# One more weight buffer, pooled group 3 in front, and the end of layer 1 in another order

## The chip, the core and the metric

The kernel runs on one core of one Trainium2 chip, alone. The metric is device time of one execution in microseconds. Three plain runs of the kernel before were timed, and one more execution was recorded by the hardware profiler. TensorE is called PE, VectorE DVE, ScalarE ACT, GpSimd POOL and SyncE SP.

## What is computed

Two layers of a diffusion backbone over 256 latent tokens and 256 context tokens of width 1024. Only the latent stream comes out, so layer 1 needs no branches or experts for the context tokens. Cut to what matters:

```python
def token_mixer(h, hc, ...):                    # four branches, each 512 wide
    out_a = fourier_mix(f_in)
    out_b = global_attention(q_b, k_b, v_b, ...)
    out_c = window_attention(q_c, k_c, v_c, ...)    # "attention c"
    out_d = pool_mix(p_in, pool_w, pool_scale)      # four groups, windows 2, 4, 8, 16
    return branch_merge(h, (out_a, out_b, out_c, out_d), ...)

def pool_mix(u, pool_w, pool_scale):
    # per group: mean over a window of tokens minus the token itself, then a 128x128 matrix
    mixed = einsum('btgc,gce->btge', pooled, pool_w)
    return mixed.reshape(b, t, POOL_W) * pool_scale

def branch_merge(h, branches, w_branch, w_gate, b_gate, w_out):
    for i, br in enumerate(branches):
        merged += sigmoid(h @ w_gate[i] + b_gate[i]) * (br @ w_branch[i])
    return merged @ w_out

def moe_ffn(h, ...):                            # 16 experts, two picked per token
    for e in range(16):
        hid = silu(tok @ w1[e]) * (tok @ w3[e])
        out += combine[:, e] * (hid @ w2[e])

def trunk_layer(...):
    x = x + g1 * token_mixer(...)
    x = x + g2 * moe_ffn(...)
# after two layers: rms_norm(x, norm_f)
```

All inputs are float32. A matmul is made of three float16 ones: the operand is split into a high and a low half, and high x high, low x high and high x low are added up.

## The kernel before

**Weights.** Every weight comes in chunks of 128 partitions by 2048 float32, 1 MB. `Stream.fill` issues their loads on SP's queue as far ahead as buffers allow. `split` makes the float16 halves: the high one (`whi`) on ACT, L319, then the low one (`wlo`) on DVE, L323; PE's three matmuls of `mm3` are L580, L581 and L582. Attention weights use the four `stage` buffers. Expert weights go round `stage`, `NEXT[l]` buffers named `ext` in the pool of the expert stage, and in layer 1 one more place (`X1`).

**The mixer.** A layer projects the inputs of attention b, runs it with the Fourier branch and `gated(0)` as filler, then does the same for attention c. Attention works through units: `S` on PE (L792, L796), the maximum on DVE (L797), the exponential `E` on ACT (L811), the row sum and `P` on ACT and DVE (L824, L825), a transpose of P by a DMA on SP's queue (L772; tiles `pair` in layer 0, `pt` in layer 1), and `po` on PE (L840). Between the steps of a unit `next(fill)` takes a step of the filler, so the order in which the filler's generators are chained sets what stands beside which unit on every engine. The filler of attention c is `spread(gated(1), pool_front(), SPREAD[l])`, then `pool_back()`, then `gated(3)`. `gated(i)` is the merge of branch i: gate matmuls (L1013 is their ACT step) and branch matmuls for two column blocks at a time. `spread` takes a step of the second generator after every step (layer 0) or every second step (layer 1) of the first.

**The pooled branch.** `pool_group(g)` computes 128 features (24 matmuls, from `h` and one half chunk of `w_in`), copies them on ACT (L941, L942), adds shifted copies on DVE (L944, L947 once for each doubling of the window, L951, L953, L955) and splits the result into `pmH` (ACT, L319) and `pmL` (DVE, L321). `mix(g)` is three matmuls with the group's matrix and the scaling into `brH`, `brL` (L975, L976). `pmH` and `pmL` have three buffers each.

**The experts.** Tokens are dealt to 16 experts in slots of 96. For each expert `up` computes w1 and w3 products (two chunks each), `hidden` their gated product `sa` (ACT L1388, DVE L1389), `down` the w2 product `py`. In layer 1 the outputs of the first fourteen experts go to DRAM (`ydram`), and when expert 14 has begun to be worked off, `fetch` gathers the rows of each token back: four indirect DMAs issued by POOL (L1405), two for each of two token tiles. `combine(t)` weighs and adds the two rows: L1412 on ACT, L1413 on DVE, and with `gated` L1415 and L1416 on DVE, which add the result to the stream X. The last two experts are added from PSUM (`acc`, L1339; their inputs `yHL`). Expert 15 keeps `sa` and its w2 chunks in float32, so its `py` matmuls (L1318) start from `sa`. In layer 0 the gathers are eight. The descriptors of POOL's indirect DMAs are built in a scratch in SBUF, whose size is an argument of the program, 16 KB a partition if none is given.

Of the kernel before, what the change touches and what calls it, by code (L numbers as in the profile page):

```python
# [23 lines left out]
NE = 16  # L24
# [13 lines left out]
BIG = 4096.0  # L38
CH = 2048
NSTG = 4  # L40
NEXT = (7, 7)
WHOLE = ((15,), (15,))
RAW = ("ada", "raw")
NWSP = 3
# [243 lines left out]
def run_all(g):  # L288
    for _ in g:
        pass  # L290
# [17 lines left out]
class Kernel:  # L308
# [305 lines left out]
    def mixer(self, l, nq, side):  # L614
        nc, tc, A, W, wk, sm = self.nc, self.tc, self.A, self.W, self.wk, self.sm
        pe, act, dve = nc.tensor, nc.scalar, nc.vector
        C, LC, split, mm3 = self.C, self.LC, self.split, self.mm3
        full = nq == NTOK
# [1 line left out]
        hH, hL = self.h if full else self.norm_mod(l, 1, NTOK, 0, 2)  # L620
        scope = ExitStack()
        at = Pool(scope.enter_context(tc.tile_pool(name=f"att{l}", bufs=1)),
                  {"pmH": 3, "pmL": 3, "a2": 3, "P": 3, "pt": 2 - full, "E": 3, "G": 2})

        def feat_part(ps, w, sl, n, k0, k1):
            mm3(ps[:, 0:n], lambda k: w[0][:, k, sl], lambda k: w[1][:, k, sl],
# [301 lines left out]
        def pool_group(g):  # L928
            w = W.get("half", "w_in", (l,), 512 + g * 128)
            ps = self.mm()  # L930
            yield from feat(ps, w, slice(0, 128), nq, True)
            pH = at.tile([128, 512], F16, "pmH")
            pL = at.tile([128, 512], F16, "pmL")
            win = POOL_WINDOWS[g]
            e = win // 2
            for st in range(nst):
                buf = [at.tile([128, T + 16], F32, f"pool{i}") for i in range(2)]
                p0 = at.tile([128, T], F32, "poolp", tag="a2")
                dve.memset(buf[0][:, 0:8], 0.0)
                dve.memset(buf[0][:, T + 8:T + 16], 0.0)  # L940
                act.activation(buf[0][:, 8:T + 8], ps[:, st * T:st * T + T], AF.Copy, scale=AS * DS)  # L941
                act.activation(p0, ps[:, st * T:st * T + T], AF.Copy, scale=AS * DS)  # L942
                cur, hi, lo, d = 1, T + 16, 1, 1
                dve.tensor_tensor(buf[1][:, 1:hi], buf[0][:, 0:hi - 1], buf[0][:, 1:hi], op=ALU.add)  # L944
                for _ in range(g):
                    nlo, nhi = lo + d, hi - d
                    dve.tensor_tensor(buf[1 - cur][:, nlo:nhi], buf[cur][:, nlo - d:nhi - d],  # L947
                                      buf[cur][:, nlo + d:nhi + d], op=ALU.add)
                    cur, lo, hi, d = 1 - cur, nlo, nhi, d * 2
                sv = buf[cur][:, 8:T + 8]  # L950
                dve.tensor_tensor(sv[:, 0:e], sv[:, 0:e], C("invc", 16 * g, 16 * g + e), op=ALU.mult)  # L951
                if e > 1:
                    dve.tensor_tensor(sv[:, T - e + 1:T], sv[:, T - e + 1:T],  # L953
                                      C("invc", 16 * g + 8, 16 * g + 7 + e), op=ALU.mult)
                dve.scalar_tensor_tensor(p0, sv, 1.0 / win, p0, op0=ALU.mult, op1=ALU.subtract)  # L955
                split(pH[:, st * T:st * T + T], pL[:, st * T:st * T + T], p0, 1.0)
                yield
            pooled[g] = pH, pL

        def pool_front():  # L960
            pool_weights()
            for g in range(3):
                yield from pool_group(g)

        def pool_back():
            bH, bL = new_br(3)
            pwH, pwL = pooled["w"]
            psl = pooled["s"]

            def mix(g):  # L970
                pH, pL = pooled.pop(g)
                po = self.mm()
                mm3(po[:, 0:nq], lambda k: pwH[:, g, :], lambda k: pwL[:, g, :],
                    lambda k: pH[:, 0:nq], lambda k: pL[:, 0:nq], 1)
                act.activation(bH[:, g, 0:nq], po[:, 0:nq], AF.Copy, scale=psl[:, g:g + 1])  # L975
                dve.scalar_tensor_tensor(bL[:, g, 0:nq], po[:, 0:nq], psl[:, g:g + 1], bH[:, g, 0:nq],  # L976
                                         op0=ALU.mult, op1=ALU.subtract)

            mix(0)
            yield  # L980
            last = pool_group(3)
            for g in range(1, 3):
                next(last, None)
                mix(g)
                yield
            yield from last
            mix(3)
            pooled["done"] = True

        mg = self.lay.tile([128, KD, nq], F32, "merged")  # L990
# [43 lines left out]
        P = project("b", 1024)  # L1034
# [3 lines left out]
        P = project("c", 1792)  # L1038
# [7 lines left out]
        self.moe_scope = ExitStack()  # L1046
        self.mp = Pool(self.moe_scope.enter_context(tc.tile_pool(name=f"moe{l}", bufs=1)), {"Dg": 1 if full else 2, "ext": NEXT[l], "yHL": 2, "whi": MORE[l], "wlo": MORE[l]})
        self.next, self.spare, self.more = NEXT[l], int(not full), MORE[l]
        self.ext = self.mp
# [30 lines left out]
    def moe(self, l, nt, side):  # L1080
        nc, tc, A, wk, sm, mp = self.nc, self.tc, self.A, self.wk, self.sm, self.mp
# [165 lines left out]
        pe_all = ntt == 2  # L1247
# [4 lines left out]
        def experts(W, hot0, h2):  # L1252
# [133 lines left out]
            def hidden(e, pa, pb):  # L1386
                sa = wk.tile([128, 4, CAP], F32, "sa", tag="t2")
                act.activation(sa, pa, AF.Silu, scale=DS)  # L1388
                dve.scalar_tensor_tensor(sa, pb, AS * DS, sa, op0=ALU.mult, op1=ALU.mult)  # L1389
                if e in whole:  # L1390
                    return sa
                hd = [wk.tile([128, 4, CAP], F16, f"hd{i}", tag="t2") for i in range(2)]
                split(hd[0], hd[1], sa, 1.0)
                return hd
# [15 lines left out]
            def combine(t, gated=False):  # L1410
                y0, y1 = mid["yg", t]
                tc.keep_in_program_order(act.activation(y0, y0, AF.Copy, scale=wr[:, 0, t:t + 1]))  # L1412
                dve.scalar_tensor_tensor(y0, y1, wr[:, 1, t:t + 1], y0, op0=ALU.mult, op1=ALU.add)  # L1413
                if gated:
                    TT(y0, y0, mid["g2"][t // 2], op=ALU.mult)  # L1415
                    TT(xt(t), xt(t), y0, op=ALU.add)  # L1416
# [33 lines left out]
            prev = more = None  # L1450
            for e in range(NE):
                pa = up(e, "w1")
                if e == NE - 1 and pe_all:
                    combine(0, True)
                if more:
                    next(more, None)
                    next(more, None)
                if prev is not None:
                    down(e - 1, prev)
                if e == NE - 1 and pe_all:  # L1460
                    combine(1, True)
                if e == NE - 1 and not pe_all:
                    fetch()
                    dw = mid["dw"] = wk.tile([128, 4, 128], F32, "dw", tag="t2")
                    for t in range(2, 4):
                        for r in range(2):
                            dve.tensor_scalar(dw[:, 2 * t - 4 + r, :], C("ident"), wr[:, r, t:t + 1], AS,
                                              op0=ALU.mult, op1=ALU.mult)
                pb = up(e, "w3")
                if e == NE - 1 and pe_all:  # L1470
                    nf = self.ext.tile([128, CH], F32, "nf", tag="ext")[:, 0:D]
                    self.row_load(nf, A["norm_f"], D)
                if more:
                    run_all(more)
                    more = None
                if pe_all and e > early:
                    for t in range(ntt):
                        for half in range(2):
                            acc[t, half] = self.ps.tile([128, 512], F32, f"acc{t}{half}", tag=("mm", "pst")[half])
                    accumulate(e - 1)  # L1480
                prev = hidden(e, pa, pb)
                if e == 1:
                    index()
                if e % EPG == 1 and e // EPG < 3:
                    more = dispatch(e // EPG + 1)
                if e == 10:
                    side_rows()
                if e == early and pe_all:
                    fetch()
# [73 lines left out]
def build(inputs):  # L1563
    import concourse.bacc as _bacc

    nc = _bacc.Bacc("TRN2", target_bir_lowering=False, num_devices=1)
    orders = {}
    Kernel(Dry(), Dry(), Dry(), orders, dry=True).body()
    arrays, A = {}, {}
    arr, places = host_arrays(inputs, orders)  # L1570
    for name, a in arr.items():
        arrays[f"in_{name}_dram"] = a
        A[name] = nc.dram_tensor(f"in_{name}_dram", a.shape, mybir.dt.from_np(a.dtype), kind="ExternalInput").ap()
    out = nc.dram_tensor("out_0_dram", (1, T, D), F32, kind="ExternalOutput").ap()
    with tile.TileContext(nc) as tc:
        Kernel(tc, A, out, orders, places).body()
    return nc, arrays
# [8 lines left out]
```

## Time and profile before

| | us |
|---|---|
| plain runs, median (lowest to highest of 3) | 1464.87 (1464.43 to 1466.42) |
| the profiled execution | 1468.68 |
| its span, from first to last instruction | 1466.9 |
| PE busy | 1352.5 (92%) |
| DVE busy | 1119.0 (76%) |
| ACT busy | 953.2 (65%) |

Layer 0 ends at about 865 us of the span. Attention c ends at about 375 in layer 0 and at about 1085 in layer 1. The rows below give all times from the start of the span. A timeline row is: start, duration, engine, line, operation, tiles, shapes, number of instructions merged, and in brackets how long the engine was idle before and what ended that. The granted clock is a share of full speed: 1.00 is 2.4 GHz and 0.50 is 1.2 GHz.

### The profile page before, as it was taken

The numbers are of one execution on the slowest core, as the hardware profiler recorded it, in microseconds if no ns is written. First come the engines' busy times: TensorE is split into PE (matmuls) and PEld (weight loads), VectorE is DVE, ScalarE is ACT, GpSimd is POOL, SyncE is SP. The second block draws the span as 40 slices with busy tenths as digits, with TensorE's granted clock in tenths as the row PEclk, the third lists the DMA queues.
The fourth block names the chain that finished last, engine by engine and source line by source line (L and its number), as shares of the span: only waits on it lengthen the run. The fifth ranks groups of instructions, "written<-read, shape, count | busy, mean of one in ns | idle before, by whom it ended". The sixth has DMA issues, their size and how long they took to land. (4 is left out here: it accounts for less than half of the span.)

```text
span 1466.9 us, 33640 instructions
## 1 busy us (share of the span) xinstructions
PE 1352.5 (92%) x14151; PEld 927.0 (63%) x14151; DVE 1119.0 (76%) x2003; ACT 953.2 (65%) x1431; POOL 14.0 (1%) x16
## 2 busy tenths in 40 slices
PE   5999999998999998999999978899989989999984
PEld 3545454444444585777777747587768767777762
DVE  3887647877354557888988888868957888989986
ACT  3777535655233337889898655856845579899971
POOL 0000000000000000000000110000000000000010
PEclk9999999999899999999999999999999999999997
DMA  9559762797685337799999564774979779999981
GB/s 365 207 131 226 228 207 87 198 232 202 187 340 191 120 111 259 270 337 419 397 420 380 222 248 177 188 234 116 232 240 361 263 280 341 418 419 419 399 327 52
DMA packets 146416, 383.31 MB, mean 261 GB/s; under 512 B 91856, under 2 KB 93904, under 8 KB 108112
## 3 DMA queue, kind: packets, MB, share of 16 engines
q1 hardware_dynamic: 133136, 355.24, 68.8%
q10 hardware_dynamic: 11392, 19.56, 3.6%
q0 software_dynamic: 1728, 6.29, 1.2%
q8 instruction: 112, 1.84, 0.5%
q14 instruction: 48, 0.39, 0.1%
HBM read 344.88 MB, written 15.20 MB: 245 GB/s over the span
## 5 line engine op out<-in xcount | busy, mean ns | idle before, releaser
L580 PE MATMUL mm<-hH,whi 128*128 128x96 f16 (+2 forms) x1824 | 398.5, 261 | 3.3 <-ACT whi L319 2.6
L582 PE MATMUL mm<-hH,wlo 128*128 128x96 f16 (+2 forms) x1824 | 398.1, 261 | 1.0 <-DVE wlo L323 0.9
L323 DVE SCALAR_TENSOR_TENSOR wlo<-stage,whi 128x1024 f16<-128x1024 f32 (+1 forms) x212 | 318.9, 1522 | 105.0 <-ACT whi L319 104.3
L581 PE MATMUL mm<-hL,whi 128*128 128x96 f16 (+2 forms) x1824 | 398.2, 261 | 0.0
L580 PEld LDWEIGHTS <-whi 128*128 128x128 f16 x3104 | 304.9, 98 | 75.2 <-issue 4.4
L319 ACT ACTIVATE whi<-stage 128x1024 f16<-128x1024 f32 (+1 forms) x212 | 269.8, 1294 | 126.2 <-PE mm L581 87.1
L582 PEld LDWEIGHTS <-wlo 128*128 128x128 f16 x3104 | 305.0, 98 | 73.7 <-DVE wlo L323 2.7
L581 PEld LDWEIGHTS <-whi 128*128 128x128 f16 x3104 | 305.0, 98 | 72.2 <-issue 2.1
L323 DVE SCALAR_TENSOR_TENSOR wlo<-ext,whi 128x2048 f16<-128x2048 f32 x116 | 262.1, 2287 | 43.2 <-ACT whi L319 43.2
L319 ACT ACTIVATE whi<-ext 128x2048 f16<-128x2048 f32 x116 | 217.8, 1904 | 9.9 <-PE mm L582 7.4
L582 PE MATMUL mm<-xg,wlo 128*128 128x96 f16 x1024 | 132.3, 206 | 0.0
L580 PE MATMUL mm<-xg,whi 128*128 128x96 f16 x1024 | 132.3, 206 | 0.0
L581 PE MATMUL mm<-xg,whi 128*128 128x96 f16 x1024 | 132.3, 206 | 0.0
L581 PE MATMUL py<-wlo,hd 128*96 128x512 f16 x240 | 90.9, 379 | 8.9 <-DVE wlo L323 8.7
L582 PE MATMUL py<-whi,hd 128*96 128x512 f16 x240 | 90.2, 381 | 6.8 <-DVE hd L321 6.0
L580 PE MATMUL py<-whi,hd 128*96 128x512 f16 x240 | 91.0, 379 | 0.0
L580 PE MATMUL mm<-brH,whi 128*128 128x512 f16 (+1 forms) x256 | 83.5, 326 | 0.0
L582 PE MATMUL mm<-brH,wlo 128*128 128x512 f16 (+1 forms) x256 | 83.4, 326 | 0.0
L581 PE MATMUL mm<-brL,whi 128*128 128x512 f16 (+1 forms) x256 | 83.4, 326 | 0.0
L1270 PE MATMUL mm<-Dg,merged 128*128 128x384 f16 x384 | 70.3, 336 | 3.8 <-DVE Dg L1203 1.8
L500 PE MATMUL mm<-stage,cpad 128*32 128x256 f32 x768 | 58.5, 408 | 13.7 <-DMA stage<-in_w_ada_dram 13.6
L825 DVE SCALAR_TENSOR_TENSOR P<-E,rl,P 128x512 f16<-128x512 f32 (+1 forms) x96 | 59.2, 659 | 8.4 <-ACT P L824 8.2
(313 smaller groups left out, 2054.2 us busy)
## 6 DMA issues: line engine op xcount, KB each, us to landing
ext<-in_w_dram SPq DMA_DIRECT2D x118, 1024.0 KB, 9.3
stage<-in_w_dram SPq DMA_DIRECT2D x62, 1024.0 KB, 9.1
stage<-in_w_ada_dram SPq DMA_DIRECT2D x48, 1024.0 KB, 6.0
stage<-in_w_gate_dram SPq DMA_DIRECT2D x32, 1024.0 KB, 5.8
stage<-in_w_in_dram SPq DMA_DIRECT2D x16, 1024.0 KB, 6.7
stage<-in_w_branch_dram SPq DMA_DIRECT2D x32, 512.0 KB, 4.1
ydram<-ys ACTq DMA_DIRECT2D x56, 192.0 KB, 6.9
stage<-in_w_out_dram SPq DMA_DIRECT2D x8, 1024.0 KB, 6.1
```

What stands on the lines that cost most here:

```text
L319: a = nc.scalar.activation(hi, src, AF.Copy, scale=scale)
L323: b = nc.vector.scalar_tensor_tensor(lo, src, scale, hi, op0=ALU.mult, op1=ALU.subtract)
L500: pe.matmul(ps[32 * j:32 * j + 32, :], self.cpad[:, 2 * k:2 * k + 32], st[:, k, :], start=k < 4, stop=k >= 4, tile_position=(0, 32 * j))
L580: pe.matmul(ps, wH(k), xH(k), start=first and k == 0, stop=False)
L581: pe.matmul(ps, wH(k), xL(k), start=False, stop=False)
L582: pe.matmul(ps, wL(k), xH(k), start=False, stop=last and k == nk - 1)
L825: dve.scalar_tensor_tensor(pv[:, 1, qt, :], E[qt][:, 0:nk], r[:, qt:qt + 1], pv[:, 0, qt, :], op0=ALU.mult, op1=ALU.subtract)
L1270: pe.matmul(ps[:, 0:SLOTS], h2[n][t][:, cs(k)], Dg[:, t].rearrange("p e c -> p (e c)"), start=t == 0, stop=t == ntt - 1)
```

## The change

Three things are changed.

1. `NEXT` goes from 7 to 8 in both layers: one more `ext` buffer, 8 KB a partition. The scratch for the descriptors of indirect DMAs goes from 16 KB to 4 KB a partition. `pmH` and `pmL` get a fourth buffer each.
2. `pool_group(3)` moves from `pool_back` to `pool_front`. Its matmuls, copies and shifts now stand among the steps of `gated(1)`, and `pool_back` is four `mix` steps and nothing else.
3. In the last expert of layer 1 `combine(0)` stands behind `down(14)` instead of ahead of it, and `combine(1)` behind `hidden(15)` instead of ahead of the w3 product.

```diff
-NEXT = (7, 7)
+NEXT = (8, 8)
...
-                  {"pmH": 3, "pmL": 3, "a2": 3, "P": 3, "pt": 2 - full, "E": 3, "G": 2})
+                  {"pmH": 4, "pmL": 4, "a2": 3, "P": 3, "pt": 2 - full, "E": 3, "G": 2})
...
         def pool_front():
             pool_weights()
-            for g in range(3):
+            for g in range(4):
                 yield from pool_group(g)
...
-            mix(0)
-            yield
-            last = pool_group(3)
-            for g in range(1, 3):
-                next(last, None)
+            for g in range(4):
                 mix(g)
                 yield
-            yield from last
-            mix(3)
             pooled["done"] = True
...
                 pa = up(e, "w1")
-                if e == NE - 1 and pe_all:
-                    combine(0, True)
...
                     down(e - 1, prev)
                 if e == NE - 1 and pe_all:
-                    combine(1, True)
+                    combine(0, True)
...
                 prev = hidden(e, pa, pb)
+                if e == NE - 1 and pe_all:
+                    combine(1, True)
...
-    nc = _bacc.Bacc("TRN2", target_bir_lowering=False, num_devices=1)
+    nc = _bacc.Bacc("TRN2", target_bir_lowering=False, num_devices=1, dynamic_dma_scratch_size=4096)
```

PE, layer 0, the last score units of attention c. `S` is a score unit, `po` the product with v, `mm<-hH,whi` a gate matmul of branch 3. Before:

```order
L796 LDWEIGHTS qs
L796 MATMUL S<-kL_2761,qs 128x256
L792 LDWEIGHTS qs
L792 MATMUL S<-kH_2760,qs 128x256
L796 LDWEIGHTS qs
L796 MATMUL S<-kL_2761,qs 128x256
L840 LDWEIGHTS vH
L840 MATMUL po<-pair,vH 64x256
L840 LDWEIGHTS vH
L840 MATMUL po<-pair,vH 64x256
```

After:

```order
L792 LDWEIGHTS qs
L792 MATMUL S<-kH_2760,qs 128x256
L796 LDWEIGHTS qs
L796 MATMUL S<-kL_2761,qs 128x256
L580 LDWEIGHTS whi
L580 MATMUL mm<-hH,whi 128x512
L792 LDWEIGHTS qs
L792 MATMUL S<-kH_2760,qs 128x256
L796 LDWEIGHTS qs
L796 MATMUL S<-kL_2761,qs 128x256
L581 LDWEIGHTS whi
L581 MATMUL mm<-hL,whi 128x512
```

The unit on kH was followed by twelve po matmuls; it now has gate matmuls inside and behind it, and its po stand some hundred rows further down. The unit on kH_2762 that follows is interleaved in the same way.

DVE, layer 1, around the last P of attention c (`pool`, `poolp` and `pmL` are those of pooled group 3). Before:

```order
L1002 SCALAR_TENSOR_TENSOR merged<-gate,merged 128x256
L323 SCALAR_TENSOR_TENSOR wlo<-stage,whi 128x1024
L825 SCALAR_TENSOR_TENSOR P<-E,rl,P 128x512 x2
L944 TENSOR_TENSOR pool_19155<-pool_19154 128x271
L976 SCALAR_TENSOR_TENSOR brL_19114<-mm,psl,brH_19113 128x256
L947 TENSOR_TENSOR pool_19154<-pool_19155 128x269
L976 SCALAR_TENSOR_TENSOR brL_19114<-mm,psl,brH_19113 128x256
L947 TENSOR_TENSOR pool_19155<-pool_19154 128x265
L323 SCALAR_TENSOR_TENSOR brL_18274<-po,brH_18273 128x256
L947 TENSOR_TENSOR pool_19154<-pool_19155 128x257
L323 SCALAR_TENSOR_TENSOR wlo<-stage,whi 128x1024
L951 TENSOR_TENSOR pool_19154<-pool_19154,cst 128x8
```

After:

```order
L996 SCALAR_TENSOR_TENSOR merged<-gate,merged 128x256
L818 TENSOR_SCALAR ls<-ls 128x2
L992 SCALAR_TENSOR_TENSOR gate<-gate,mm 128x256
L820 RECIPROCAL rl<-ls 128x2
L976 SCALAR_TENSOR_TENSOR brL_19163<-mm,psl,brH_19162 128x256
L996 SCALAR_TENSOR_TENSOR merged<-gate,merged 128x256
L976 SCALAR_TENSOR_TENSOR brL_19163<-mm,psl,brH_19162 128x256 x2
L825 SCALAR_TENSOR_TENSOR P<-E,rl,P 128x512 x2
L323 SCALAR_TENSOR_TENSOR brL_18274<-po,brH_18273 128x256
L976 SCALAR_TENSOR_TENSOR brL_19163<-mm,psl,brH_19162 128x256
L323 SCALAR_TENSOR_TENSOR wlo<-stage,whi 128x1024 x3
```

The shifts of group 3 no longer follow the last P; they stand ahead of it, among the operations of the two units before. Two of the brL operations that stood between the shifts stand ahead of the last P now.

DVE, layer 1, the tail (`sa` is expert 15's hidden product, L1413 is now L1407, L1415 L1409, L1416 L1410 and L1389 L1383; `wlo<-X` before and the last `wlo<-ext` after are the low half of the last w3 chunk). Before:

```order
L323 SCALAR_TENSOR_TENSOR wlo<-ext,whi 128x2048 x2
L1413 SCALAR_TENSOR_TENSOR yg<-yg,wr 128x1024
L323 SCALAR_TENSOR_TENSOR yHL<-py,slotw,yHL 96x512
L1415 TENSOR_TENSOR yg<-yg,merged 128x1024
L323 SCALAR_TENSOR_TENSOR wlo<-X_24636,whi 128x2048
L1416 TENSOR_TENSOR X_4729<-X_4729,yg 128x1024
L323 SCALAR_TENSOR_TENSOR yHL<-py,slotw,yHL 96x512
L1413 SCALAR_TENSOR_TENSOR yg<-yg,wr 128x1024
L1389 SCALAR_TENSOR_TENSOR sa<-mm,sa 128x384
L1415 TENSOR_TENSOR yg<-yg,merged 128x1024
```

After:

```order
L323 SCALAR_TENSOR_TENSOR wlo<-stage,whi 128x2048
L1291 TENSOR_TENSOR slotw<-slotw_25129 96x1
L323 SCALAR_TENSOR_TENSOR wlo<-ext,whi 128x2048
L323 SCALAR_TENSOR_TENSOR yHL<-py,slotw,yHL 96x512 x2
L1407 SCALAR_TENSOR_TENSOR yg<-yg,wr 128x1024 x2
L1409 TENSOR_TENSOR yg<-yg,merged 128x1024
L1383 SCALAR_TENSOR_TENSOR sa<-mm,sa 128x384
L1410 TENSOR_TENSOR X_4729<-X_4729,yg 128x1024
L1409 TENSOR_TENSOR yg<-yg,merged 128x1024
L1290 TENSOR_SCALAR slotw_25303<-mm 96x2
L1410 TENSOR_TENSOR X_4729<-X_4729,yg 128x1024
```

The last split stood behind the first weighted row pair, which waits for the gathers, and stands ahead of it now. `sa` stood behind four operations of the two combines and a fifth, L1416, of the first one; now behind both L1407 and one L1409. On ACT the two L1406 stand together behind the split of the last chunk, where the first L1412 stood ahead of it.

## Rows read from the trace of the kernel before

**Rows 1.** Busy time in a stretch: us, PE, PEld, DVE, ACT, POOL, clock, DMA share, GB/s.
```profile
1300.00:1393.00 93.00, 89.12 (x1354) 71.44 (x1353) 86.62 (x50) 84.89 (x80) 0.00 (x0) 1.00 1.01 413
```

**Rows 2.** Grouped instructions, experts of layer 1, 1200 to 1416: high halves of fetched chunks.
```profile
L319 ACT ACTIVATE whi<-ext 128x2048 f16<-128x2048 f32 x47 | 88.1, 1906 | 0.8 <-ACT ys L1333 0.4 <-ACT sa L1388 0.4
```

**Rows 3.** Busy time by stretch, layer 0, end of the second attention.
```profile
356.00:360.00 4.00, 2.41 (x36) 1.73 (x33) 2.70 (x11) 1.29 (x3) 0.00 (x0) 1.00 0.75 246
360.00:364.00 4.00, 0.50 (x3) 0.30 (x3) 3.14 (x11) 3.92 (x12) 0.00 (x0) 0.61 1.11 135
364.00:368.00 4.00, 2.40 (x15) 1.27 (x14) 4.00 (x15) 1.78 (x6) 0.00 (x0) 0.50 0.28 56
368.00:372.00 4.00, 2.31 (x6) 0.80 (x6) 3.12 (x10) 2.81 (x9) 0.00 (x0) 0.50 0.87 222
372.00:376.00 4.00, 4.00 (x15) 1.50 (x13) 0.84 (x2) 0.00 (x0) 0.00 (x0) 0.68 1.13 264
```

**Rows 4.** Timeline of PE, same place: start, duration, instruction, idle before and its releaser.
```profile
363.50 0.37 PE L792 MATMUL S<-kH,qs 128*128 128x256 f16 x1 [5.09 <-ACT E L811]
```

**Rows 5.** Timeline of ACT, same place.
```profile
359.40 1.06 ACT L319 ACTIVATE whi<-stage 128x1024 f16<-128x1024 f32 x1 [2.71 <-DMA stage<-in_w_gate_dram]
```

**Rows 6.** Busy time by stretch, layer 1, end of the second attention.
```profile
1060.00:1070.00 10.00, 5.92 (x66) 5.03 (x64) 10.00 (x24) 7.52 (x17) 0.00 (x0) 1.00 0.96 255
1070.00:1080.00 10.00, 7.59 (x51) 5.78 (x51) 2.22 (x4) 1.36 (x3) 0.00 (x0) 0.66 0.53 153
1080.00:1090.00 10.00, 10.00 (x98) 8.68 (x96) 5.34 (x8) 4.17 (x6) 0.00 (x0) 1.00 0.48 158
```

**Rows 7.** Timeline of PE, same place.
```profile
1072.41 0.42 PE L840 MATMUL po<-pt,vH 128*64 128x256 f16 x2 [6.50 <-DMA pt<-P]
```

**Rows 8.** Timelines of ACT (one row) and DVE (three), the tail.
```profile
1433.69 1.15 ACT L1412 ACTIVATE yg<-yg,wr 128x1024 f32<-128x1024 f32 x1 [2.35 <-DMA yg<-ydram,late]
...
1432.52 1.29 DVE L1413 SCALAR_TENSOR_TENSOR yg<-yg,wr 128x1024 f32<-128x1024 f32 x1 [6.74 <-DMA yg<-ydram,late]
...
1434.38 1.21 DVE L1415 TENSOR_TENSOR yg<-yg,merged 128x1024 f32<-128x1024 f32 x1
...
1441.75 0.56 DVE L1389 SCALAR_TENSOR_TENSOR sa<-mm,sa 128x384 f32<-128x384 f32 x1 [0.97 <-PE mm L582]
```

**Rows 9.** Timeline of POOL: first and last gather of layer 0, all four of layer 1.
```profile
838.78 1.07 POOL L1405 DMA_INDIRECT yg<-ydram,late  x1 [838.33 <-DVE dw L1467]
...
847.60 0.94 POOL L1405 DMA_INDIRECT yg<-ydram,late  x1 [0.30 <-issue]
1421.95 2.44 POOL L1405 DMA_INDIRECT yg<-ydram,late  x1 [573.41 <-DMA stage<-in_w_dram]
1424.69 1.90 POOL L1405 DMA_INDIRECT yg<-ydram,late  x1 [0.30 <-DMA yg<-ydram,late]
1426.90 0.94 POOL L1405 DMA_INDIRECT yg<-ydram,late  x1 [0.30 <-issue]
1428.14 0.94 POOL L1405 DMA_INDIRECT yg<-ydram,late  x1 [0.30 <-issue]
```

**Rows 10.** The queue of the gathers (packets, MB, share), and their issues (median us to landing).
```profile
q0 software_dynamic: 1728, 6.29, 1.2%
...
yg<-ydram,late POOLq DMA_INDIRECT x12, 6.7
```

**Rows 11.** Timeline of DVE, layer 1, just behind the last P.
```profile
1065.97 0.43 DVE L944 TENSOR_TENSOR pool<-pool 128x271 f32<-128x271 f32 x1
1066.33 0.48 DVE L976 SCALAR_TENSOR_TENSOR brL<-mm,psl,brH 128x256 f16<-128x256 f32 x1
1066.72 0.43 DVE L947 TENSOR_TENSOR pool<-pool 128x269 f32<-128x269 f32 x1
```

**Rows 12.** Busy time by stretch, the tail, around the start of the py matmuls.
```profile
1440.00:1443.00 3.00, 3.00 (x25) 2.05 (x23) 2.03 (x3) 0.00 (x0) 0.00 (x0) 0.52 0.00 0
1443.00:1446.00 3.00, 3.00 (x8) 1.14 (x7) 1.77 (x4) 0.00 (x0) 0.00 (x0) 1.00 0.00 0
```

## The prediction

> **What bounds the kernel now.** I read the slices of the page first, then busy time by stretch, then the timeline inside each stretch where TensorE (PE) is idle. PE is the engine that sets the time: in the expert stretch of layer 1 it is busy 89.12 of 93 us, and the same stretch keeps DVE at 86.62, ACT at 84.89 and the DMA engines at a share of 1.01, 413 GB/s [rows 1]. So four resources are nearly equal there, and which of them ends last is read from what ACT waits for before it splits a fetched chunk into its high half: 0.8 us in all for 47 chunks, and none of it a DMA [rows 2]. The weights are there before they are wanted. Outside the experts PE has three holes, and the change touches the place of each:
> - Layer 0, end of the second attention, 356 to 376: PE idle 1.59 + 3.50 + 1.60 + 1.69 = 8.4 us, and a granted clock of 0.61 and 0.50 (1.2 GHz is 0.50) while it works again [rows 3]. The longest hole, 5.09 us, waits for ACT's exponentials [rows 4], and ACT had stood 2.71 us in front of a gate weight that was still on its way [rows 5].
> - Layer 1, the same place: PE idle 4.08 + 2.41 us, and a clock of 0.66 in the ten microseconds behind it [rows 6]. The hole is one wait of 6.50 us for a transpose of the last P [rows 7].
> - The tail: DVE and ACT stand before gathered rows, and the last weight split stands behind them [rows 8].
>
> **The change part by part.**
>
> Eighth buffer. It removes nothing and lets one more 1 MB chunk be in flight. Since a missing chunk costs ACT nothing now [rows 2], I take 0. The bound below zero: if the DMA engines at 413 GB/s were what ends last [rows 1], 1.05 MB earlier gives 1.05 / 0.413 = 2.5 us a layer, 5 us in two. The bound above: the same chunk now runs 2.5 us beside the loads issued then, and one of them is late by that, +2.5. The fourth pmH and pmL buffers only make room for the fourth pooled group; they cost no time on any engine.
>
> Descriptor scratch, 16 KB to 4 KB. Only the twelve gathers use it. Their issue takes 0.94 us when nothing disturbs it [rows 9], they land 6.7 us after issue [rows 10], and eight of them follow each other at (847.60 - 838.78) / 7 = 1.26 us, so five are in flight at once without a wait. What a quarter of the space holds, no row shows; I take 0, and the price of the other case is a rival below. The Trainium skill, "DMA: Bandwidth & Descriptors", in its sections on terms and on SWDGE, has 16-byte descriptors in rings across 16 partitions; by it 4 KB a partition would be 256 of them a ring, an estimate, against 1728 / 12 / 16 = 9 packets [rows 10] that a gather puts on each DMA engine, so it would bind nobody. No run here shows that yet.
>
> Pooled group 3 moves to the front: layer 0. The 24 feature matmuls, the group's ACT copies and DVE shifts leave the last stretch, and run earlier, among the gate matmuls of branch 1. That work is not saved: everything between the two places is later by as much as it takes, and the last stretch is shorter by the same. What changes is what stands beside the last score units. Before, the last two follow each other with only po matmuls between; now gate matmuls of branch 3 stand between and behind them (order, above). The hole's worth: 8.4 us idle, and of the work done at a low clock 0.50 x 0.39 + 2.40 x 0.50 + 2.31 x 0.50 + 4.00 x 0.32 = 3.8 us [rows 3], so 12.2. Not all goes: the gate weight that feeds the filler is asked for by SP behind two transposes, as now, and ACT's split of it stands ahead of the last unit's exponentials. ACT lost 2.71 us there before [rows 5]; I put the rest at that to 4 us of PE idle and 1 to 2 us of clock, 5.7 together. Gain 12.2 - 5.7 = 6.5. Bounds: 11.7, if the load comes in time, and 3, if the hole stays as one wait as long as the 5.09 [rows 4] and keeps its clock loss.
>
> The same move in layer 1. Here DVE is full (10.00 of 10) until the last P [rows 6], so eight DVE operations of the group, which now follow the last P, and two brL operations come before it. At the pace of those rows, 0.36 us for each of the larger [rows 11], that is about 2.3 + 0.8 = 3.1 us: the last P is ready 3.1 us later, and its transposed copy at 1072.4 + 3.1 = 1075.5 instead of 1072.4 [rows 7]. PE itself arrives at that wait no later, because the group's matmuls are only moved, and now finds 63 matmuls ahead of the waiting po (3 mix, 48 gate, 12 branch). At 10.00 us for 98 [rows 6] they are 6.4 us: from 1065.9 to 1072.3. What is left is 3.2 us of idle. Before, the hole was 6.5 us and 7.59 x 0.34 = 2.6 us of clock [rows 6]: 9.1. Gain 9.1 - 3.2 = 5.9; a little clock may still be lost, so 5.5. The SP queue has the same transposes and gate loads in both, and what is queued behind the later transpose is one gate load. Bounds: 9, if the DVE delay is hidden as well; 2, if the filler waits for its own weights.
>
> The end order. Before, ACT's first multiplication of gathered rows stood ahead of the split of the last chunk; now both combines stand behind it, so PE gets the last w3 chunk without a stop. But hidden's sa now stands in DVE's queue behind both gathered multiplications and one gate product. ACT's second multiplication starts at 1433.69 and takes 1.15 us, then 1.29 and 1.21 us on DVE: 1437.3 for sa, against 1441.75 now [rows 8], 4.4 us earlier. Two things take from it. First, the third gather. The two that were issued beside DVE's splits took 2.44 and 1.90 us, the two beside an idle DVE 0.94 [rows 9]; the split of the last chunk now runs to about 1428, over the third one (1426.90), so it and what waits for it are some 1.2 us later: 3.2. The Trainium skill, "SBUF — State Buffer", section "Who interferes with whom", has a DVE instruction with two SBUF inputs contend with a GpSimd instruction that reads SBUF; by that the third gather waits until the split has ended, 1428 + 0.94 instead of 1427.8, which the two long issues bear out. Without the rule the term would be 4.4. Second, the clock. Before, the last chunk's matmuls brought PE back to full speed (0.52, then 1.00) as the py matmuls began [rows 12]. Now PE is idle for some 6 us before sa and starts py cold; a hole of 6.5 us cost 2.6 us in layer 1, so I take 2. py is on the path. Gain 3.2 - 2.0, and I take 1.5; bounds 4.4 and 0.
>
> **Sum.** 6.5 + 5.5 + 1.5 = 13.5 us. The profiled execution is 1468.68 us, of which 1466.9 is span; it goes to 1455.2. It lies 3.8 us over the median of the runs, 1464.87, and no term depends on that, so the time is 1464.87 - 13.5 = 1451.4.
>
> **The rivals.**
> - The holes close only in part: both attention ends at their lower bounds, tail 1: 3 + 2 + 1 = 6, 1459. For it: each has a weight load close behind the transposes [rows 5]. Against it: both have more filler than before.
> - The DMA engines did end last among the experts, so the eighth buffer adds its 5 us: 1446.4. For it: a share of 1.01 [rows 1]. Against it: ACT waits for no chunk [rows 2].
> - The work moves and the waits move with it, as the filler is bought from the stretch before: within 2 us of 1464.9. Against it: before the hole of layer 0 no engine is full.
> - Slower: the smaller ring holds one gather. Then each is issued when the last has landed: in layer 0 7 x 6.7 = 47 us instead of 8.8 [rows 9, 10], +38, in layer 1 3 x 6.7 = 20 instead of 6.2, +14; less 13.5 that is 1503. With room for two the last of layer 0 starts 20 us after the first, +11, and layer 1 pays about 2: 1464. So it decides below two gathers. Against it: five were in flight in four times the space.
>
> **How the numbers follow.** Chances: the forecast 0.62, in part 0.15, DMA 0.08, waits that move 0.08 (a ring for two gathers is in it), a ring for one 0.07. The forecast's own spread is about 1446 to 1457; with the part case and the DMA case the range is 1443 to 1461. A measurement here tells some 0.2% from no change, 2.9 us. Faster than 1461.9: 0.62 + 0.15 + 0.08 = 0.85; same 0.08; slower 0.07.
>
> **What would show it.** Layer 0: PE idle between 350 and 376 below 4 us, clock near 1.00. Layer 1: the wait of po for pt under 3.5 us, later by some 3 us. Tail: no wait of PE for the last whi, sa about 3 us sooner against py's neighbours, py at a clock near 0.5. Experts: the same busy time by stretch. Gathers: issue times of 0.94 to 2.4 us; one of 6 us would make the prediction wrong, and so would a PE wait for a gate weight of over 5 us in either attention.

## The result and the profile after

The changed kernel takes 1449.62 us (median of 4 runs, 1445.61 to 1454.27) against 1465.52 for the kernel before, in the same comparison: a ratio of 0.9893, 95% interval 0.9862 to 0.9924. That is 15.9 us, where 13.5 had been forecast. The profiled execution took 1450.25 us, with a span of 1448.5.

The page shows that no engine got less to do:

```profile
PE 1348.9 (93%) x14151; PEld 925.3 (64%) x14151; DVE 1118.5 (77%) x2003; ACT 952.9 (66%) x1431; POOL 15.6 (1%) x16
```

PE's 1352.5 us have become 1348.9; the span is 18.4 shorter. What has gone is time in which PE waited or ran at half clock. The numbers below are read at four places, in the order of the prediction. Behind `pool_back`, lines of the code have moved up by 6 to 8 against the kernel before.

**Experts.** The stretch of layer 1 that answers to [rows 1] (same columns), 15 us sooner, and the row that answers to [rows 2]:

```profile
1285.00:1378.00 93.00, 89.13 (x1355) 71.39 (x1354) 86.62 (x50) 84.92 (x80) 0.00 (x0) 1.00 1.01 411
...
L319 ACT ACTIVATE whi<-ext 128x2048 f16<-128x2048 f32 x48 | 89.8, 1909 | 0.0
```

PE, DVE and ACT are as busy as before to within 0.04 us, and ACT still waits for no chunk. From the first w1 matmul of layer 1's experts to the first w3 matmul of expert 10 are 159.6 us (1175.72 to 1335.35); before also 159.6 (1190.86 to 1350.49). The eighth buffer changes nothing here. Below, "expert 10's w3" is the mark from which the tail is measured.

**Attention c of layer 0.** Busy time by stretch, for [rows 3]; the PE row with the longest wait that is left, for [rows 4]; and ACT's two waits for a gate weight, for [rows 5]:

```profile
340.00:356.00 16.00, 14.96 (x119) 7.51 (x119) 12.01 (x36) 9.50 (x26) 0.00 (x0) 1.00 0.73 205
356.00:360.00 4.00, 4.00 (x29) 2.14 (x28) 3.86 (x15) 2.45 (x10) 0.00 (x0) 1.00 0.94 365
360.00:364.00 4.00, 2.80 (x15) 1.35 (x14) 2.81 (x9) 3.80 (x9) 0.00 (x0) 1.00 0.97 218
364.00:368.00 4.00, 4.00 (x34) 1.71 (x33) 3.50 (x13) 2.96 (x9) 0.00 (x0) 1.00 0.59 179
368.00:372.00 4.00, 4.00 (x28) 1.94 (x27) 1.47 (x4) 1.29 (x3) 0.00 (x0) 1.00 1.16 294
372.00:376.00 4.00, 4.00 (x35) 1.70 (x34) 2.26 (x3) 1.67 (x3) 0.00 (x0) 1.00 0.71 131
```

```profile
362.26 0.27 PE L792 MATMUL S<-kH,qs 128*128 128x256 f16 x1 [1.20 <-ACT E L811]
```

```profile
336.06 2.00 ACT L319 ACTIVATE whi<-stage 128x1024 f16<-128x1024 f32 x2 [3.19 <-DMA stage<-in_w_gate_dram]
...
359.91 1.06 ACT L319 ACTIVATE whi<-stage 128x1024 f16<-128x1024 f32 x1 [1.04 <-DMA stage<-in_w_gate_dram]
```

PE's idle time from 356 to 376 is 1.2 us instead of 8.4, and the clock is 1.00 throughout. ACT's wait at the old place (359.91) has shrunk from 2.71 to 1.04 us. A longer one stands at 336.06, one gate load earlier, where before ACT had not waited; PE has enough queued to run through it in this execution. In the second profiled execution of the same kernel (e8_change_again) ACT waits 3.91 us there and PE 0.53, so that PE runs through is not sure.

**Attention c of layer 1**, for [rows 6] and [rows 7]:

```profile
1050.00:1060.00 10.00, 10.00 (x110) 8.15 (x109) 9.82 (x23) 8.56 (x18) 0.00 (x0) 1.00 0.83 231
1060.00:1070.00 10.00, 9.45 (x96) 8.05 (x94) 7.07 (x10) 4.28 (x6) 0.00 (x0) 1.00 1.01 279
```

```profile
1063.68 0.38 PE L840 MATMUL po<-pt,vH 128*64 128x256 f16 x3 [0.56 <-DMA pt<-P]
```

The wait of po for the last transpose is 0.56 us instead of 6.50, and the clock is 1.00 in both rows. DVE is full to 9.82 where it was full to 10.00, and has 7.07 us of work behind it where it had 2.22. The last P on DVE and its transpose on SP's queue, first before, then after:

```profile
1064.65 1.41 DVE L825 SCALAR_TENSOR_TENSOR P<-E,rl,P 128x512 f16<-128x512 f32 x2
...
1066.09 4.20 SPq L772 DMA_TRANSPOSE pt<-P  x1
```

```profile
1057.06 1.41 DVE L825 SCALAR_TENSOR_TENSOR P<-E,rl,P 128x512 f16<-128x512 f32 x2 [0.18 <-ACT P L824]
...
1058.50 3.23 SPq L772 DMA_TRANSPOSE pt<-P  x1
```

Before, P ended (1066.06) 0.15 us after PE had come to the wait (1065.91). Now it ends (1058.47) 4.65 us ahead of PE (1063.12), and DVE waits 0.18 us for ACT's half of P, so DVE's own queue no longer holds it up.

**The tail.** The four gathers, for [rows 9]; on DVE the split of the last w3 chunk and sa, for [rows 8]; and the first twelve py matmuls on PE, before and after, with the stretch that they begin in:

```profile
1407.07 2.17 POOL L1399 DMA_INDIRECT yg<-ydram,late  x1 [568.31 <-PE hotT L1294]
1409.54 1.97 POOL L1399 DMA_INDIRECT yg<-ydram,late  x1 [0.30 <-DMA yg<-ydram,late]
1411.81 1.96 POOL L1399 DMA_INDIRECT yg<-ydram,late  x1 [0.30 <-ACT yHL L319]
1414.08 0.94 POOL L1399 DMA_INDIRECT yg<-ydram,late  x1 [0.30 <-issue]
```

```profile
1410.68 2.28 DVE L323 SCALAR_TENSOR_TENSOR wlo<-ext,whi 128x2048 f16<-128x2048 f32 x1
...
1421.69 0.55 DVE L1383 SCALAR_TENSOR_TENSOR sa<-mm,sa 128x384 f32<-128x384 f32 x1
```

```profile
1442.41 5.60 PE L1318 MATMUL py<-stage,sa 128*96 128x512 f32 x12
...
1422.30 7.25 PE L1312 MATMUL py<-ext,sa 128*96 128x512 f32 x12 [4.60 <-DVE sa L1383]
...
1422.00:1425.00 3.00, 2.70 (x4) 0.99 (x5) 3.00 (x5) 0.00 (x0) 0.00 (x0) 0.50 0.00 0
```

The last split (1410.68 to 1412.96) lies over the third gather, which took 1.96 us instead of 0.94. Since the shift up to the experts is 15.1 us, sa at 1421.69 answers to 1436.8, 4.9 us sooner than 1441.75. PE waits 4.60 us for it and takes 7.25 us for twelve py matmuls that took 5.60 before, at a clock that is 0.50 from 1422 to 1425.

### The profile page after: what moved, and what is told of

It reads as the page before. It is cut to its first block, busy times and chain, and to the rows that moved or that the text cites. A ratio compares the mean times of both kernels' runs of the same rounds, so it can differ in the third digit from the quotient of the medians.

```text
span 1448.5 us, 33643 instructions
## 1 busy us (share of the span) xinstructions
PE 1348.9 (93%) x14151; PEld 925.3 (64%) x14151; DVE 1118.5 (77%) x2003; ACT 952.9 (66%) x1431; POOL 15.6 (1%) x16
## 5 line engine op out<-in xcount | busy, mean ns | idle before, releaser
L323 DVE SCALAR_TENSOR_TENSOR wlo<-stage,whi 128x1024 f16<-128x1024 f32 (+1 forms) x208 | 310.0, 1507 | 101.2 <-ACT whi L319 100.5
L319 ACT ACTIVATE whi<-stage 128x1024 f16<-128x1024 f32 (+1 forms) x208 | 262.0, 1282 | 121.4 <-PE mm L581 84.8
L323 DVE SCALAR_TENSOR_TENSOR wlo<-ext,whi 128x2048 f16<-128x2048 f32 x121 | 272.4, 2285 | 42.3 <-ACT whi L319 42.3
L319 ACT ACTIVATE whi<-ext 128x2048 f16<-128x2048 f32 x121 | 227.1, 1905 | 12.8 <-PE mm L582 10.8
```

Of the source, the lines that this page charges most:

```text
L319: a = nc.scalar.activation(hi, src, AF.Copy, scale=scale)
L323: b = nc.vector.scalar_tensor_tensor(lo, src, scale, hi, op0=ALU.mult, op1=ALU.subtract)
```

## The experiments

Times are medians; the kernel before ran beside each, with medians of 1465.85 to 1466.16.

### The parts alone

**The ring alone** (e1_ring): the kernel before with

```diff
-NEXT = (7, 7)
+NEXT = (8, 8)
...
+    ... dynamic_dma_scratch_size=4096)
```

> The kernel before with the eighth buffer and the 4 KB scratch alone. Theory (experts are bound by PE, DVE and ACT together, chunks wait for ACT): 1465.5, within 1.5 us; busy time of PE in the expert stretch of layer 1 and ACT's idle before the split of a fetched chunk as before. Rival, the DMA engines end last there: 2.5 us a layer, 1460.5. Rival, the smaller ring holds gathers up: gathers of layer 0 start more than 1.3 us apart and the time goes up by 11 us or more.

Measured: 1463.4 us, ratio 0.9978 (0.9968 to 0.9988), 2.5 us off (1465.89), and neither expectation fits. The experts take 159.6 us, as before. The gain stands in the tail. DVE, end of layer 1:

```profile
1424.11 2.28 DVE L323 SCALAR_TENSOR_TENSOR wlo<-ext,whi 128x2048 f16<-128x2048 f32 x1
...
1429.98 1.28 DVE L1413 SCALAR_TENSOR_TENSOR yg<-yg,wr 128x1024 f32<-128x1024 f32 x1 [3.59 <-DMA yg<-ydram,late]
...
1435.97 0.55 DVE L1389 SCALAR_TENSOR_TENSOR sa<-mm,sa 128x384 f32<-128x384 f32 x1
```

The low half of the last w3 chunk (1424.11) stands ahead of the first weighted pair (1429.98), as in the changed kernel, though no combine was moved. With eight buffers in the round the last expert's chunks fall into other places (in the kernel before the last one is `wlo<-X`), and the program that sets the order of each engine put its split first. The kernel of e5_scratch (next) differs from this one in `NEXT` alone and has the old order, so the number of buffers is what changed it; that it does so by way of the place is read from the tile names and wasn't tried by itself. From expert 10's w3 to sa are 85.5 us instead of 91.3, and to the end of the span 112.7 instead of 116.4.

**The scratch alone** (e5_scratch): the kernel before with `dynamic_dma_scratch_size=4096`. The order of every engine is that of before.

> The kernel before with the 4 KB scratch and nothing else; every engine has the order of before. Theory (the smaller ring holds the gathers): 1465.9 within 1 us, gathers of layer 0 some 1.25 us apart and issued in 0.93 to 1.1 us. Rival (the scratch, and not the buffer, is what took 2.5 us off in the run of both): 1463.4.

Measured: 1465.41 us, ratio 0.9997 (0.9989 to 1.0006). The last two gathers of layer 0 on POOL:

```profile
847.19 0.93 POOL L1405 DMA_INDIRECT yg<-ydram,late  x1 [0.30 <-issue]
...
848.43 0.94 POOL L1405 DMA_INDIRECT yg<-ydram,late  x1 [0.30 <-issue]
```

They are 1.24 us apart and issued in 0.93 and 0.94 us, as in the larger space [rows 9]. A quarter of the scratch costs nothing for eight gathers in a row.

**The end order alone** (e3_tail): the kernel before with the two combines moved, nothing else.

```diff
-                if e == NE - 1 and pe_all:
-                    combine(0, True)
...
                 if e == NE - 1 and pe_all:
-                    combine(1, True)
+                    combine(0, True)
...
                 prev = hidden(e, pa, pb)
+                if e == NE - 1 and pe_all:
+                    combine(1, True)
```

> The kernel before with the two combines of layer 1's last expert moved, nothing else. Theory: sa 4.5 to 5 us sooner, py matmuls started cold and 1.7 us longer, so 3.2 us, 1462.3. Rival, the gathers' landing sets the end, so that nothing but the wait moves: 1465.5.

Measured: 1465.61 us, ratio 0.9998 (0.9985 to 1.001): no gain that can be told. The interval goes from 2.2 us faster to 1.5 us slower. In its trace sa comes 4.5 us sooner, counted from expert 10's w3, and the py matmuls take most of that back:

```profile
1436.54 8.31 PE L1318 MATMUL py<-stage,sa 128*96 128x512 f32 x12 [5.71 <-DVE sa L1389]
```

PE waits 5.71 us and then runs twelve py matmuls in 8.31 us, 2.7 more than in the kernel before. From expert 10's w3 to the end are 114.5 us in this trace; five traces with seven buffers and the old end order (before, e5, e6, e7, e2) have 115.1 to 116.4. So 0.6 to 1.9 us are left in the trace, which the medians neither show nor exclude.

**The pooled group in front** in both layers (e2_front), in layer 0 alone (e6_front_l0) and in layer 1 alone (e7_front_l1), each with four pmH and pmL buffers:

```diff
-            for g in range(3):
+            for g in range(4 if l == 0 else 3):     # e6; l == 1 in e7; 4 in e2
                 yield from pool_group(g)
```

and `pool_back` of the changed kernel in the same layers.

> The kernel before with pooled group 3 in front and four pmH, pmL buffers, nothing else. Theory (the two attention ends give 11.3 and 7.5 us, as the trace of the change has it, and the routing behind them loses up to 4 us of TensorE's clock): 1465.5 - 18.8 + 0 to 4 = 1446.7 to 1450.7. Rival, the eighth buffer is what fills those holes by loading earlier: less than 8 us of gain here.

> The kernel before with pooled group 3 in front in layer 0 alone. Theory: the end of attention c in layer 0 gives 11 us (PE idle there 8.4 to about 2 us, clock back at 1.00), the rest stays: 1455. Rival (the waits of layer 0 come back as waits behind it): under 6 us, 1460 or more.

> The kernel before with pooled group 3 in front in layer 1 alone. Theory: the wait of 6.5 us for the last transpose falls below 1 us and the clock behind it returns, 7 us, of which the routing's clock takes 0 to 3: 1459 to 1462. Rival (DVE, full to the last P, is later by what was put ahead of it and PE waits for that): 0 to 2 us, 1464 or more.

Measured: both 1453.97, ratio 0.9914 (0.9897 to 0.9932), 11.9 us; layer 0 alone 1459.7, 0.9952 (0.9939 to 0.9965), 6.2 us; layer 1 alone 1459.0, 0.996 (0.9947 to 0.9972), 6.9 us. The two layers add up to 13.1 us, both together give 11.9. What I expected after having seen the trace of the change was too much for both (18.8 less at most 4) and for layer 0 (11): 1459.7 lies 0.3 us from the rival's 1460 and 4.7 from the theory. Layer 1 came out at the lower end of its theory, 1459. The trace of before, against which I had measured, is itself an execution 2.8 us over its median. The trace of layer 0 alone shows where its gain goes. It is 10.3 us ahead of the trace of before at the first normalising matmul of layer 0's experts (543.30 against 553.58) and 6.1 at expert 10's w3 of layer 1: 1.4 us are lost in the routing of layer 0 (mean clock 0.90 instead of 0.95), 1.4 in the mixer of layer 1 and 1.4 in the routing of layer 1 (0.80 instead of 0.93). At the new place ACT waits 4.72 us, and PE 1.34 of them:

```profile
337.15 2.00 ACT L319 ACTIVATE whi<-stage 128x1024 f16<-128x1024 f32 x2 [4.72 <-DMA stage<-in_w_gate_dram]
```

In layer 1 alone the stretch that answers to [rows 6] has no hole, and a clock of 1.00:

```profile
1060.00:1070.00 10.00, 10.00 (x101) 8.32 (x98) 8.68 (x20) 8.01 (x17) 0.00 (x0) 1.00 0.99 244
...
1070.00:1080.00 10.00, 9.18 (x94) 7.88 (x93) 5.53 (x8) 3.79 (x6) 0.00 (x0) 1.00 0.99 348
```

The traces of all kernels but e9_warm, which adds matmuls, give the two attention ends by themselves. The first normalising matmul of layer 0's experts starts at 550.5 to 554.4 us in the five with the old order of layer 0, and at 542.3 to 548.2 in the six with the new one: 8.4 us apart in the mean. From the first normalising matmul of layer 1's mixer to that of its experts are 296.0 to 299.3 us in the five with the old order of layer 1, and 289.7 to 293.9 in the six with the new one: 6.7 apart. The wait of po for the last transpose is 5.91 to 6.50 us in the former and 0.24 to 0.85 in the latter.

### The ring taken out of the change

e10_no_ring is the changed kernel with `NEXT = (7, 7)` and the full scratch.

> The changed kernel without the eighth buffer and with the full scratch. Theory (the buffer gives nothing among the experts; what it gave alone was the order of the tail, which the moved combines give as well): within 1.5 us of the changed kernel. Rival (it gives 2.5 us wherever it is): 2.5 us slower than the changed kernel.

Measured: 1452.75 us, ratio to before 0.9903 (0.9883 to 0.9923); the changed kernel, run beside it, 1449.88 with 0.9899 (0.9879 to 0.9919). The medians are 2.9 us apart, the intervals nearly the same, so the times don't tell the two expectations apart. The traces put the answer between them: from expert 10's w3 to the end are 114.1 us here, 113.1 and 112.0 in the two executions of the changed kernel, so beside the moved combines the eighth buffer is worth 0.9 to 2.1 us. Its profiled execution shows something else, at the new wait of layer 0 (ACT, then PE):

```profile
341.68 2.00 ACT L319 ACTIVATE whi<-stage 128x1024 f16<-128x1024 f32 x2 [6.65 <-DMA stage<-in_w_gate_dram]
...
344.78 0.37 PE L792 MATMUL S<-kH,qs 128*128 128x256 f16 x1 [3.27 <-ACT E L811]
```

The order of the mixer in layer 0 is that of the changed kernel, where the same wait was 3.19 us and PE didn't stop; here it is 6.65, and PE stops for 3.27. That the missing buffer causes this isn't shown. In the six traces with this order of layer 0 ACT's wait is 3.15 us (e2, seven buffers), 3.19 and 3.91 (the changed kernel twice), 4.48 (e4), 4.72 (e6, seven buffers) and 6.65 (e10), and PE's part of it 0, 0, 0.53, 1.30, 1.34 and 3.27. Why the load is late by such different amounts stays open.

### The same kernel again

e8_change_again is the changed kernel itself.

> The changed kernel itself, for its spread and as the neighbour of the next two. 1449.6 by its first runs; theory (TensorE's clock falls in the waits of the routing in some executions and not in others): runs spread over 5 us or more, the slower ones with the lower mean clock.

Measured: 1449.88 us, from 1447.22 to 1455.6, with mean clocks that go from 0.985 to 0.979 in the same order. The routing of layer 1 shows what differs. Busy time by stretch (columns as in [rows 1]), first the profiled execution of the change, then that of this run:

```profile
1148.00:1152.00 4.00, 2.88 (x16) 2.69 (x17) 3.72 (x15) 1.52 (x3) 0.00 (x0) 0.70 1.01 424
1152.00:1156.00 4.00, 4.00 (x24) 3.94 (x24) 3.25 (x11) 2.08 (x5) 0.00 (x0) 0.50 0.66 240
...
1164.00:1168.00 4.00, 1.09 (x10) 0.68 (x10) 3.73 (x27) 1.70 (x3) 0.00 (x0) 0.83 0.99 303
1168.00:1172.00 4.00, 4.00 (x15) 1.80 (x13) 3.52 (x20) 1.68 (x4) 0.00 (x0) 0.50 0.99 410
1172.00:1176.00 4.00, 4.00 (x26) 2.23 (x25) 2.70 (x9) 2.32 (x5) 0.00 (x0) 0.81 0.66 277
```

```profile
1148.00:1152.00 4.00, 2.73 (x15) 2.35 (x16) 3.72 (x22) 1.58 (x1) 0.00 (x0) 0.74 0.98 389
1152.00:1156.00 4.00, 4.00 (x43) 3.97 (x42) 3.96 (x11) 3.31 (x7) 0.00 (x0) 0.84 0.71 254
...
1164.00:1168.00 4.00, 1.87 (x13) 1.05 (x13) 3.86 (x30) 1.13 (x5) 0.00 (x0) 0.87 0.90 291
1168.00:1172.00 4.00, 4.00 (x18) 2.08 (x17) 3.70 (x16) 2.38 (x5) 0.00 (x0) 0.70 0.98 412
1172.00:1176.00 4.00, 4.00 (x65) 3.21 (x63) 3.64 (x12) 1.49 (x5) 0.00 (x0) 1.00 0.51 213
```

The code is the same and the waits start within 1 us of each other. The clock was 0.50 from 1152 to 1156 in one and 0.84 in the other, 0.50 against 0.70 from 1168 to 1172. From the first normalising matmul to the first w1 matmul of the experts were 27.2 us in the first and 24.3 in the second; in the kernel before 24.0. PE's idle time in them is 4.5, 4.1 and 4.8 us, its mean clock 0.75, 0.86 and 0.93: the time differs by the clock. The 27.2 are the longest of all twelve traces of this case, where the others have 23.8 to 25.5.

### PE kept busy in the routing

e9_warm has sa in front (e4, below) and matmuls that nobody reads, where PE waits in the routing:

```diff
+        if n == 2:
+            self.warm(24)       # ahead of the normalising matmuls
...
+        self.warm(40)           # ahead of the matmuls that number the tokens
         pp = self.mm((128, ntt + 1, 16))
```

> The kernel with sa in front, with 24 and 40 small matmuls more in the routing of each layer that nobody reads, placed where PE waits for DVE (1.06 and 2.27 us in layer 1). Theory (the 3 us that the changed kernel gives back between 1146 and 1190 are a low clock, for the waits there are the same as before): clock 1.00 in the routing of both layers, some 3 us off, 1438 to 1440, with a smaller spread. Rival (something else is late there, so the added work only costs): 1441.9 to 1445.

Measured: 1445.82 us, ratio 0.9863 (0.9845 to 0.9882), against 1441.87 without them: the gain of the theory isn't there, and the time is 0.8 us over what the rival allowed. The clock did what the theory says, in layer 1, though PE is idle for 2.2 of the 4 us from 1170 to 1174:

```profile
1170.00:1174.00 4.00, 1.79 (x17) 1.05 (x16) 3.83 (x28) 1.42 (x5) 0.00 (x0) 1.00 0.95 289
...
1174.00:1178.00 4.00, 3.18 (x18) 1.64 (x17) 3.90 (x18) 2.10 (x5) 0.00 (x0) 1.00 1.00 420
```

But the routing from the first normalising matmul on takes 23.8 us, and with 1.3 us of added matmuls ahead of that 25.1, against 24.6 in the trace without them. In these executions there were not 3 us to get back. In layer 0 of this profiled execution PE also stopped 2.48 us behind the gate weight. Why the median is 3.9 us higher isn't settled by that: the order of other engines changed with the added instructions as well.

### sa ahead of the gathered rows

e4_sa_first is the changed kernel with both combines behind `hidden(15)` and their DVE multiplications bound to that order:

```diff
-                if e == NE - 1 and pe_all:
-                    combine(0, True)
...
                 if e == NE - 1 and pe_all:
+                    combine(0, True)
                     combine(1, True)
...
+                keep = tc.keep_in_program_order if gated else (lambda i: i)
-                dve.scalar_tensor_tensor(y0, y1, ...)
+                keep(dve.scalar_tensor_tensor(y0, y1, ...))
...
+                if e == NE - 1 and pe_all:
+                    tc.keep_in_program_order(last)      # sa of expert 15
```

> The changed kernel with both combines behind hidden(15) and their DVE multiplications kept in program order, so that sa stands ahead of both on DVE. Theory (sa behind the gathered rows is what PE waits for, 4.6 us, and the cold clock of py costs 1.7): sa ready with the last w3 matmul, PE without that wait, py at full clock, 5 to 6 us off the changed kernel, about 1444. Rival (the gathers and the DVE work behind them set the end whatever sa does): within 1 us of the changed kernel, 1449.6.

Measured: 1441.87 us (1439.62 to 1443.46), ratio to before 0.9832 (0.9818 to 0.9846), some 8 us under the changed kernel and the fastest of all. DVE and PE in its tail:

```profile
1414.78 0.56 DVE L1383 SCALAR_TENSOR_TENSOR sa<-mm,sa 128x384 f32<-128x384 f32 x1 [0.64 <-PE mm L582]
...
1416.07 1.28 DVE L1410 SCALAR_TENSOR_TENSOR yg<-yg,wr 128x1024 f32<-128x1024 f32 x1 [0.73 <-DMA yg<-ydram,late]
...
1416.51 5.34 PE L1312 MATMUL py<-ext,sa 128*96 128x512 f32 x12
```

sa follows the last w3 matmul after 0.64 us and doesn't wait for the gathered rows, whose first weighted pair comes behind it at 1416.07. PE goes from the last w3 matmul through the added outputs to py without a stop, and the twelve py matmuls take 5.34 us at full clock instead of 7.25. From expert 10's w3 to the end of the span are 105.5 us (105.1 in e9_warm, which has the same end order), against 113.1 and 112.0 in the changed kernel and 116.4 before. The place of `combine(0)` and the bound order of DVE were changed together and weren't tried apart.

## Why the prediction came out

The time, 1449.6 against 1451.4, and the sign were right. Alone, its parts gave 6.2 (layer 0), 6.9 (layer 1), 2.5 (ring) and 0.3 us (end order), 15.9 in all, and the whole change gave 15.9. That the two agree so closely is luck: each part is known to 1.5 to 2.6 us, and the two layers together gave 11.9 where their sum is 13.1. In the tail the ring alone (112.7 us from expert 10's w3) does as much as ring and end order together (113.1 and 112.0). Against the forecast the parts are off by +2.5 (ring), +1.4 (layer 1), -1.2 (end order) and -0.3 us (layer 0), which in part cancel. By its own steps:

- **What bounds the kernel**: right. Three holes of PE were the place, and the experts' 159.6 us didn't move.
- **Scratch, 0**: right (e5_scratch), and with it the rival of a ring too small is gone. The estimate made from the Trainium skill, "DMA: Bandwidth & Descriptors", section "Terms" (16-byte descriptors), that 4 KB would bind nobody agrees with it: eight gathers went through at the old spacing. No run here shows how large a descriptor is.
- **Eighth buffer, 0**: the reason was right and the term was wrong. It gives nothing by loading earlier, and 2.5 us by changing the order. The step that failed is the claim that it "removes nothing": with another number of buffers the last chunk falls into another place and its split stands elsewhere in DVE's order. I had seen in the order of the changed kernel that the last `wlo` came from `ext` and no longer from X, and put the whole move down to the combines.
- **Layer 0, 6.5**: 6.2 alone. The hole closed more than I had said: idle 8.4 to 1.2 us and all of the clock, 11.0 in this pair of traces, and the stage behind it starts 8.4 us sooner in the mean of eleven. Two steps failed. I had put the rest of the wait at the old place, where ACT's wait fell to 1.04 us; the longer one stands at the gate load before it, at 336, where it is 3.15 to 6.65 us in six traces and stops PE for 0 to 3.27. My rival of holes that close only in part named a late weight load, but another one. And I had let the gain arrive whole at the end of the layer and beyond: in the trace of layer 0 alone 4.2 of 10.3 us are given back behind it.
- **Layer 1, 5.5**: 6.9 alone. Of the 3.2 us of wait that were to remain 0.56 did. Counted from the layer's first normalising matmul (868.97 and 858.83), PE came to the wait 7.35 us later than before (6.4 forecast), the last P ended 2.55 later (3.1), and from the transpose's start to the use of its rows were 5.18 us, where I had carried over 6.32 from before: 0.95 + 0.55 + 1.14 = 2.64. The filler was mis-sized as much as the transpose.
- **End order, 1.5**: 0.3 alone, between the bounds, with 1.5 inside the interval. sa came 4.5 us sooner instead of 3.2, and the cold py cost 2.7 instead of 2.0.
- **The third gather**: its issue as forecast, its effect not. It took 1.96 us beside the split (2.56 in e3_tail), 0.94 beside an idle DVE. This agrees with the Trainium skill, "SBUF — State Buffer", section "Who interferes with whom": the split reads two tensors in SBUF, and the gather waited, to 0.8 us behind the split's end. But what waits for it was not 1.2 us later: from the start of its issue to ACT's second multiplication are 6.70 us in e3_tail (1425.55 to 1432.25) and 6.79 before (1426.90 to 1433.69).
- **"Experts: the same busy time"** held, "no wait of PE for the last whi" held, "py at a clock near 0.5" held, "one of 6 us" among the gather issues did not occur. "PE idle between 350 and 376 below 4 us" held: from 340 on it is 1.04 + 1.20 = 2.2.

What the prediction didn't have is the give-back in the routing: 18.4 us of lead at the first normalising matmul of layer 1's experts have become 15.1 at the first w1 matmul. That is the clock: in the second execution of the same kernel the routing takes 24.3 us, so the give-back isn't bound to the change.

## What to carry to other kernels

A filler that is only moved paid twice here: it filled the wait that it went to, and kept the matmul clock up behind it. Look, at the same time, at the load that feeds it one step earlier, since the next wait stood there, and at the stages behind, which gave part of the gain back. The size of a ring can change the order in which a scheduler lays out work that has nothing to do with bandwidth, so run such a part alone before giving its gain to the edit that looks responsible. And where the last stage waits for two things, put the one that starts the longer chain first in the queue that both share: here that was worth some 8 us on top of the change, whose own moves in the tail, end order and ring, had given 2.8.

## What the runs showed of the hardware

- The granted clock behind the same short waits differs from execution to execution of the same kernel: 0.50 against 0.84 in the routing of layer 1, and the routing takes 27.2 or 24.3 us. Ten runs of the changed kernel spread over 10.0 us (1445.61 to 1455.6); the slower ones have, by and large, the lower mean clock (0.985 in the two fastest, 0.979 to 0.981 in the three slowest). 23 runs of the kernel before spread over 6.4.
- An indirect DMA issued on POOL took 0.94 us beside an idle DVE and 1.90 to 2.56 us where it began while DVE split a chunk (two SBUF operands, 2.28 us each), in every kernel of this study in which the two met; it then ended 0.8 us behind the end of the split in which it began. In layer 0 of the changed kernel a gather that began 0.47 us into a DVE multiplication of two SBUF tensors (L1407, 835.42) took 1.62 us; in the kernel before one that began 0.04 us ahead of it (L1413, 846.40) took 0.93.
- Twelve fp32 matmuls of 512 columns took 5.34 to 5.95 us when PE came to them busy and 7.25 to 8.31 us after a wait of 4.60 to 5.75 us (7.34 in e1_ring, after two waits of 2.56 and 1.20).
